# A bidirectional delta-rule scan: the two directions on separate rows of the array, four heads in one chain

## The chip, the core and the metric

The kernel runs on one core of a Trainium2 chip. Its engines are named as the profile names them: PE is TensorE (matrix products; PEld are its weight loads), DVE is VectorE, ACT is ScalarE, POOL is GpSimd, SP is SyncE. The metric is the time of one execution on the device in microseconds (us), the median of several executions; lower is better.

## What is computed

The reference is a trunk of two layers over 512 tokens of 2048 channels in float32. Each layer normalises its input, projects it by one large product, and runs two mixers beside each other: a gated delta rule in both directions over the tokens, 8 heads of 128 channels (the mixer that the change touches), and a diagonal state-space branch. Both are gated, projected, merged and projected back onto the residual.

The delta rule goes over the tokens in 8 chunks of 64. With the state S (128 x 128 for each head and direction), the triangular systems of a chunk solved beforehand, and the decays folded into the operands, one chunk is:

```python
v_new = u_c - w_c @ S                     # new values
o_c   = (q_c * exp(g)) @ S + qk_c @ v_new # outputs of the chunk
S     = S * exp(g_last) + (k_c * exp(g_last - g)).T @ v_new
...
out   = forward(q, k, v) + flip(backward(flip(q), flip(k), flip(v)))
```

## The kernel before

Activations lie channel by channel: a tile is [128 channels, 512 tokens]. The large products keep weights stationary and stream the tokens. Each float32 operand there is split into two parts, hi and lo, and a product is three instructions per contraction tile (`_steps`, lines 122 to 124, output `acc`). The parts of the weights are made by `_split`: a cast to w_hi on ACT (line 65) and a subtract to w_lo on DVE (line 66), each over 1024 columns.

The scan, `_delta_scan`, is the serial part. It runs in 16 steps per layer: two groups of four heads (hg), 8 chunks each (j); I count the steps of a layer from 0 to 15. In a step the forward direction takes chunk j and the backward direction chunk 7 - j. A chunk fills 64 of 128 rows: `half[d]` is the half of the rows in which direction d's chunk lies, and the two directions always lie in opposite halves, which change places from step to step. Before the change the four heads of a group are two chains x of two heads, and each step has these pieces:

- **ps_T** (line 807): keys and queries times the old state, for each direction and head over all 128 rows. Then r_s on DVE (line 810), v minus that, for one half at a time, and the decay of the state on DVE (line 813).
- **ps_V** (line 821): the solved triangle t_b times r_s, both directions at once. ACT copies each half into tiles v_z of its own (line 824), which are zero in the other direction's half.
- **ps_S** (line 831): the state update, tokens as contraction. All 128 rows are used, the other direction's rows of v_z being zero. DVE adds it to the state (line 836); in chunk 0 ACT copies it (line 834).
- **ps_T again** (line 839): the chunk's inner outputs are added onto the same PSUM tile, 64 columns of the array for each direction. ACT copies the result to o_tok in the first half of the chunks (line 844), DVE adds it there in the second (line 846).

Chunk 0 has no ps_T product at first, chunk 7 no state update. A float32 product of this size is two instructions on PE.

To cover the waits between the pieces, `fill.run(FILL)` puts three contraction tiles of dense products (nine instructions) between them, at three places in each step. The fills take their work from a generator: first the two last tiles of the input projection, then the eight products of the state branch's gate, then its projection. When one of the gate's products ends, ACT takes the sigmoid (line 1097), DVE multiplies twice (glu_s, line 1098; z_in, line 1099), and the result is split again (a cast on ACT, and a subtract named act on DVE, lines 65 and 66). A product of the gate has 8 contraction tiles and a step takes 9, so the ends wander through the steps.

After chunk 7 of a group, `norm` normalises the outputs of its heads on DVE and ACT; the transposes of one head at a time (ps_o) are put behind the next steps.

The order on PE within the scan is that of the code; on DVE, ACT, POOL and SP a scheduler sets it ahead of time by its own estimate, and each engine takes its instructions strictly in that order. The loads of a step (keys, values, triangles) go through POOL's DMA queue one step ahead. The PSUM pool has one buffer for each of the tiles T0, T1 (ps_T) and W0, W1 (ps_V and ps_S in turn), so a new ps_T waits until the outputs of the step before have been read.

Of the kernel before, what the change touches and what calls it, by code (L numbers as in the profile page):

```python
# [24 lines left out]
D = 2048  # L25
# [22 lines left out]
# The order of the first three products.  x: loads an input tile; h: its two parts; s: its squares;  # L48
# w j,k,n: weights of product j from contraction tile k on; p j,n: the next n steps of product j.
# [10 lines left out]
def _bc(ap, shape):  # L60
    return ap.to_broadcast(shape)
# [7 lines left out]
def _rsqrt(nc, pool, out, a, tag, bufs=None):  # L69
    """out = a ** -0.5: table root, exact reciprocal, one Newton step."""  # L70
# [32 lines left out]
class _Fill:  # L103
    """Dense products in small steps, for the places where another chain waits."""
# [11 lines left out]
def _steps(c, acc, nk, unit, hi, lo):  # L116
    """acc = w.T @ act, one contraction tile at a time; unit gives the weights from a tile on."""
# [17 lines left out]
def _sum_sq(c, ps, acc, t0, n, first):  # L135
    """Adds the sums of acc over partitions, token tiles t0 to t0 + n, onto the columns of ps [token, tile]."""
# [13 lines left out]
def _spread(c, pb, r, n):  # L150
    """pb [any partition, token] = r [token, tile]."""
# [4 lines left out]
def _rstd(c, acc, out):  # L156
    """out = (sum of acc over partitions / D + eps) ** -0.5 on every partition."""
# [8 lines left out]
def _scaled_parts(c, x, g, hi, lo):  # L166
    """Splits x*g into hi, lo."""
# [4 lines left out]
def _add_squares(c, pool, k, x, acc):  # L172
    """Adds x*x onto acc."""
# [29 lines left out]
# ---------------------------------------------------------------- decay rows  # L203
# [1071 lines left out]
```

## Time and profile before

| | us |
|---|---|
| median of 3 executions | 3102.58 (3101.16 to 3102.80) |
| the profiled execution, first to last instruction (span) | 3099.7 |
| PE busy | 3049.4 |
| DVE busy | 2307.3 |
| ACT busy | 1049.6 |
| POOL busy | 425.6 |

For the profiled execution the trace gives its span alone; the executions that are timed without the profiler have a median 2.9 us above it. Instructions on PE are pipelined, so that the durations of neighbours overlap; what a burst costs is read from start to start, or from the chain of waits, which gives each piece its own stretch. The scan of layer 0 lies at 1020 to 1216 us, that of layer 1 at 2560 to 2760 us.

### The profile page before, as it was taken

To read this page: it belongs to the slowest core of one execution; us is meant where nothing else is said; L and a number is where in the kernel's file an instruction comes from. 1 tells how busy PE (TensorE), PEld (TensorE's weight loads), DVE (VectorE), ACT (ScalarE), POOL (GpSimd) and SP (SyncE) were. 2 spreads that over 40 slices of the span, in tenths; PEclk is the share of its full clock that TensorE was granted. 3 is DMA by queue.
4 is the path that set the end of the run, shared out by engine and by line. 5 is a ranking of instruction groups with operands and counts; after the bars stand their busy time and mean duration, and the time that the engine had idled before them with its cause. 6 is when DMAs were issued, how large, how long until landed. Compare 5 with 4: busy or idle time off the path is not lost.

```text
span 3099.7 us, 45254 instructions
## 1 busy us (share of the span) xinstructions
PE 3049.4 (98%) x17142; PEld 2442.4 (79%) x17142; DVE 2307.3 (74%) x4455; ACT 1049.6 (34%) x1441; POOL 425.6 (14%) x706
## 2 busy tenths in 40 slices
PE   9999999999999999999999999999999999999998
PEld 7777788777887888888887677877778878888887
DVE  8899969997797586543487998889959965765433
ACT  4343344333222442322223334343332224423222
POOL 1010112212101231000010102022130012300000
PEclk9999999999999999999999999999999999999999
DMA  6343446755434765754433435466564356657433
GB/s 204 93 140 105 129 153 179 214 168 157 153 119 149 223 195 178 245 169 143 148 112 96 129 103 150 137 195 193 166 181 139 119 188 191 201 187 232 154 117 114
DMA packets 199289, 493.47 MB, mean 159 GB/s; under 512 B 58336, under 2 KB 62912, under 8 KB 198048
## 3 DMA queue, kind: packets, MB, share of 16 engines
q1 hardware_dynamic: 154416, 345.84, 35.1%
q0 software_dynamic: 44512, 144.74, 15.3%
q8 instruction: 135, 2.21, 0.3%
q14 instruction: 82, 0.67, 0.1%
q10 hardware_dynamic: 144, 0.01, 0.0%
HBM read 381.64 MB, written 108.86 MB: 158 GB/s over the span
## 4 chain that ended last, share of the span: by engine, by line
PE 83%; DVE 11%; issue 3%; DMA 1%; ACT 0%; POOL 0%; SPq 0%; POOLq 0%; DVEq 0%; ACTq 0%
PE acc L122 24%; PE acc L123 24%; PE acc L124 24%; DVE w_lo L66 2%; PE ps_y L271 2%; PE ps_S L831 2%; PE ps_T L807 1%; DVE st_b L482 1%; DVE st_b L481 1%; DVE h_st L484 1%; PE ps_e L271 1%; DVE cv_y L550 1%; PE ps_et L457 1%; PE ps_T L839 1%; DVE st_a L483 1%
## 5 line engine op out<-in xcount | busy, mean ns | idle before, releaser
L122 PE MATMUL acc<-act,w_hi 128*128 128x512 f32 x3200 | 1279.0, 400 | 5.5 <-DVE cv_pre L546 3.7
L124 PE MATMUL acc<-act,w_lo 128*128 128x512 f32 x3200 | 1271.6, 397 | 3.5 <-DVE w_lo L66 3.5
L123 PE MATMUL acc<-act,w_hi 128*128 128x512 f32 x3200 | 1269.6, 397 | 0.0
L65 ACT CAST w_hi<-w_raw 128x1024 fp32r<-128x1024 f32 (+1 forms) x467 | 488.2, 1046 | 1202.1 <-PE acc L123 879.9
L66 DVE TENSOR_TENSOR w_lo<-w_raw,w_hi 128x1024 fp32r<-128x1024 f32 (+1 forms) x465 | 566.7, 1219 | 266.5 <-ACT w_hi L65 264.3
L122 PEld LDWEIGHTS acc<-act,w_hi 128*128 128x128 f32 x3200 | 603.0, 188 | 150.4 <-issue 8.4
L124 PEld LDWEIGHTS acc<-act,w_lo 128*128 128x128 f32 x3200 | 602.7, 188 | 149.4 <-issue 7.0
L123 PEld LDWEIGHTS acc<-act,w_hi 128*128 128x128 f32 x3200 | 603.3, 189 | 138.4 <-issue 5.1
L122 PE MATMUL acc<-m_l,w_hi 128*128 128x512 f32 (+1 forms) x528 | 205.0, 388 | 0.0
L123 PE MATMUL acc<-m_h,w_hi 128*128 128x512 f32 (+1 forms) x528 | 204.8, 388 | 0.0
L124 PE MATMUL acc<-m_h,w_lo 128*128 128x512 f32 (+1 forms) x528 | 204.7, 388 | 0.0
L550 DVE SCALAR_TENSOR_TENSOR cv_y<-cv_pre,cw,cv_y 128x510 f32<-128x510 f32 (+1 forms) x192 | 142.6, 746 | 7.5 <-ACT cv_y L548 5.5
L122 PEld LDWEIGHTS acc<-m_l,w_hi 128*128 128x128 f32 x528 | 99.5, 188 | 21.9
L123 PEld LDWEIGHTS acc<-m_h,w_hi 128*128 128x128 f32 x528 | 99.5, 188 | 21.8
L124 PEld LDWEIGHTS acc<-m_h,w_lo 128*128 128x128 f32 x528 | 99.5, 188 | 21.8
L693 DVE TENSOR_TENSOR x_tmp<-x_inv 128x62 f32<-128x62 f32 (+30 forms) x124 | 106.3, 857 | 2.9
L695 DVE TENSOR_TENSOR x_inv<-x_inv,x_tmp 128x62 f32<-128x62 f32 (+30 forms) x124 | 106.3, 857 | 2.7
L1072 DVE TENSOR_TENSOR z_t<-acc,rstd_b 128x512 f32<-128x512 f32 x96 | 66.0, 687 | 48.2 <-PE acc L124 47.6
L1158 DVE TENSOR_TENSOR x_res<-x_res,acc 128x512 f32<-128x512 f32 x31 | 21.3, 687 | 103.7 <-PE acc L124 86.5
L1142 DVE TENSOR_TENSOR g_in<-acc,g_in 128x512 f32<-128x512 f32 x32 | 22.1, 692 | 79.4 <-PE acc L124 79.4
L518 POOL DMA_DIRECT2D m_l<-d_k x128 | 67.3, 534 | 82.2 <-PE ps_y L271 56.1
L484 DVE TENSOR_TENSOR h_st<-h_st,st_a 128x64 f32<-128x64 f32 x256 | 70.3, 275 | 5.1
(356 smaller groups left out, 3251.0 us busy)
## 6 DMA issues: line engine op xcount, KB each, us to landing
w_raw<-in_w_in_dram SPq DMA_DIRECT2D x319, 512.0 KB, 4.0
w_raw<-in_w_out_dram SPq DMA_DIRECT2D x64, 512.0 KB, 3.9
d_keqe<-k_e POOLq DMA_DIRECT2D x32, 512.0 KB, 4.5
d_g<-z_t SPq DMA_DIRECT2D x64, 256.0 KB, 2.1
w_raw<-in_w_pb_dram SPq DMA_DIRECT2D x32, 512.0 KB, 3.7
g_in<-d_g SPq DMA_DIRECT2D x64, 256.0 KB, 3.1
w_raw<-in_w_pa_dram SPq DMA_DIRECT2D x32, 512.0 KB, 4.3
ke_s<-d_keqe POOLq DMA_DIRECT2D x56, 256.0 KB, 4.1
```

What stands on the lines that cost most here:

```text
L65: nc.scalar.copy(out=hi, in_=src)
L66: nc.vector.tensor_tensor(out=lo, in0=src, in1=hi.bitcast(F32), op=ALU.subtract)
L122: c.nc.tensor.matmul(acc, wh[:, q, :], lo(k), start=k == 0, stop=False)
L123: c.nc.tensor.matmul(acc, wh[:, q, :], hi(k), start=False, stop=False)
L124: c.nc.tensor.matmul(acc, wl[:, q, :], hi(k), start=False, stop=k == nk - 1)
L271: c.nc.tensor.matmul(out[r], w[:, r], x, start=start, stop=stop)
L484: V.tensor_tensor(out=hs(n + 1), in0=hs(n + 1), in1=a, op=ALU.add)
L518: c.q.dma_start(out=M[s_ * 16:(s_ + 1) * 16].rearrange("p g t c -> p g (t c)"), in_=c.d_k[l][j][:, :, 0:16, (7 - s_) * 16:(15 - s_) * 16]. ...
L550: nc.vector.scalar_tensor_tensor(out=y[:, o0:o1], in0=pre[:, i0:i0 + o1 - o0], scalar=cw[:, tap:tap + 1], in1=y[:, o0:o1], op0=ALU.mult, o ...
L693: V.tensor_tensor(out=t, in0=_bc(X[:, k + 1:, k:k + 1], [128, n, k]), in1=_bc(X[:, k:k + 1, 0:k], [128, n, k]), op=ALU.mult)
L695: V.tensor_tensor(out=X[:, k + 1:, 0:k], in0=X[:, k + 1:, 0:k], in1=t, op=ALU.add)
L1072: V.tensor_tensor(out=z, in0=acc, in1=c.rstd, op=ALU.mult)
```

## The change

Three things change in `_delta_scan`, and `norm` is written for the new tiles.

1. The two chains of two heads become one of four. The tiles of the state, of r_s, of the new values, of ps_T, ps_V and ps_S now hold four heads, and each step issues half as many instructions on DVE and ACT, of twice the columns.
2. The state product and the inner outputs take only the 64 rows in which the direction's chunk lies (`half[d]`), so that the two directions stand on different rows of the array. The zeroed tiles v_z and their memsets go; ps_V is copied in one piece to v_n.
3. ps_T and ps_S have a PSUM bank for each direction. The banks in use stay four: two for T, two for W.

The number of products is the same. Comments and docstrings are gone from the whole file, which moves line numbers: line 836 of before is 821 after, 846 is 831, 810 is 803, 831 is 817, 839 is 824.

```diff
     V = nc.vector
     HL = [slice(0, 64), slice(64, 128)]
-    NC = 2
+    H4 = 4
     with ExitStack() as es:
         psp = es.enter_context(tc.tile_pool(name=f"sps_{l}", bufs=1, space=PSUM, reuse_waits="tile"))
         tp = es.enter_context(tc.tile_pool(name=f"st_{l}", bufs=1, side="right", reuse_waits="tile"))
         wk = es.enter_context(tc.tile_pool(name=f"sw_{l}", bufs=2, side="right", reuse_waits="tile"))
-        tb = [tp.tile([128, 4, 128], F32, name=f"t_b{q}") for q in range(2)]
-        # new values, zero in the half of the other direction
-        vz = [[[tp.tile([128, 2, 128], F32, name=f"v_z{x}{d}{p}") for p in range(2)] for d in range(2)] for x in range(NC)]
-        Sg = [[tp.tile([128, 2, 2, 128], F32, name=f"s_st{hg}{x}") for x in range(NC)] for hg in range(2)]
-        og = [[tp.tile([128, 4, 2, 128], F32, name=f"o_tok{hg}{x}") for x in range(NC)] for hg in range(2)]
-        for q in tb + [vz[x][d][p] for x in range(NC) for d in range(2) for p in range(2)]:
+        tb = [tp.tile([128, H4, 128], F32, name=f"t_b{q}") for q in range(2)]
+        Sg = [tp.tile([128, 2, H4, 128], F32, name=f"s_st{hg}") for hg in range(2)]
+        og = [tp.tile([128, 4, H4, 128], F32, name=f"o_tok{hg}") for hg in range(2)]
         def norm(hg):
...
+            ot = og[hg]
+            ms = tp.tile([128, 4, H4], F32, name=f"o_ms{hg}")
...
         late = []
         ahead = load(*steps[0])
         for s, (hg, j) in enumerate(steps):
             S, ot = Sg[hg], og[hg]
-            p = j % 2
             n_, t_, half = where(j)
             T, ke, ld = ahead
             if s + 1 < len(steps):
                 ahead = load(*steps[s + 1])
-            pT, rr, vv = [], [], []
-            for x in range(NC):
-                g0 = hg * 4 + 2 * x
-                ps = psp.tile([128, 2, 2, 128], F32, name=f"ps_T{x}", tag=f"T{x}")
-                r = wk.tile([128, 2, 128], F32, name=f"r_s{x}", tag=f"r_s{x}", bufs=1)
+            hs = slice(hg * 4, hg * 4 + 4)
+
+            ps = psp.tile([128, 2, H4, 128], F32, name="ps_T", tag="T")
+            r = wk.tile([128, H4, 128], F32, name="r_s", tag="r_s", bufs=1)
+            for d in range(2):
                 if j == 0:
-                    # the state is zero
+
+                    V.tensor_copy(out=r[half[d]], in_=ld[d][2][half[d]])
+                else:
+                    for h in range(H4):
+                        nc.tensor.matmul(ps[:, d, h, :], ke[d][:, h, :], S[:, d, h, :],
+                                         start=h == 0, stop=True, skip_group_check=True)
+                    V.tensor_tensor(out=r[half[d]], in0=ld[d][2][half[d]], in1=ps[half[1 - d], d], op=ALU.subtract)
+            if 0 < j < NCH - 1:
+                V.tensor_tensor(out=S, in0=S, in1=_bc(c.egl[:, :, hs, j:j + 1], [128, 2, H4, 128]), op=ALU.mult)
+            fill.run(FILL)
+            pv = psp.tile([128, H4, 128], F32, name="ps_V", tag="W")
+            for h in range(H4):
+                nc.tensor.matmul(pv[:, h, :], T[:, h, :], r[:, h, :], start=True, stop=True)
+            vv = wk.tile([128, H4, 128], F32, name="v_n", tag="v_n")
+            nc.scalar.copy(out=vv, in_=pv)
+            fill.run(FILL)
+            if j < NCH - 1:
+                pS = psp.tile([128, 2, H4, 128], F32, name="ps_S", tag="W")
+                for h in range(H4):
                     for d in range(2):
-                        V.tensor_copy(out=r[half[d]], in_=ld[d][2][half[d], 2 * x:2 * x + 2])
+                        nc.tensor.matmul(pS[:, d, h, :], ld[d][1][half[d], h, :], vv[half[d], h, :], start=True, stop=True)
+                if j == 0:
+                    nc.scalar.copy(out=S, in_=pS)
                 else:
-                    for d in range(2):
-                        for h in range(2):
-                            nc.tensor.matmul(ps[:, d, h, :], ke[d][:, 2 * x + h, :], S[x][:, d, h, :],
-                                             start=d == 0 and h == 0, stop=True, skip_group_check=True)
-                    for d in range(2):
-                        V.tensor_tensor(out=r[half[d]], in0=ld[d][2][half[d], 2 * x:2 * x + 2],
-                                        in1=ps[half[1 - d], d], op=ALU.subtract)
-                    if j < NCH - 1:
-                        V.tensor_tensor(out=S[x], in0=S[x], op=ALU.mult,
-                                        in1=_bc(c.egl[:, :, g0:g0 + 2, j:j + 1], [128, 2, 2, 128]))
-                pT.append(ps)
-                rr.append(r)
-            fill.run(FILL)
-            for x in range(NC):
-                pv = psp.tile([128, 2, 128], F32, name=f"ps_V{x}", tag=f"W{x}")
-                for h in range(2):
-                    nc.tensor.matmul(pv[:, h, :], T[:, 2 * x + h, :], rr[x][:, h, :], start=True, stop=True)
-                vv.append([vz[x][d][p] for d in range(2)])
+                    V.tensor_tensor(out=S, in0=S, in1=pS, op=ALU.add)
+            for h in range(H4):
                 for d in range(2):
-                    nc.scalar.copy(out=vv[x][d][half[d]], in_=pv[half[d]])
-            fill.run(FILL)
-            for x in range(NC):
-                if j < NCH - 1:
-                    ps = psp.tile([128, 2, 2, 128], F32, name=f"ps_S{x}", tag=f"W{x}")
-                    for d in range(2):
-                        for h in range(2):
-                            nc.tensor.matmul(ps[:, d, h, :], ld[d][1][:, 2 * x + h, :], vv[x][d][:, h, :],
-                                             start=True, stop=True)
-                    if j == 0:
-                        nc.scalar.copy(out=S[x], in_=ps)
-                    else:
-                        V.tensor_tensor(out=S[x], in0=S[x], in1=ps, op=ALU.add)
-                for h in range(2):
-                    for d in range(2):
-                        nc.tensor.matmul(pT[x][half[d], d, h, :], ld[d][0][:, 2 * x + h, :],
-                                         vv[x][d][:, h, :], start=j == 0 and h == 0, stop=True, skip_group_check=True)
-                for d in range(2):
-                    o = ot[x][half[d], t_[d]]
-                    if j < NCH // 2:
-                        nc.scalar.copy(out=o, in_=pT[x][half[d], d])
-                    else:
-                        V.tensor_tensor(out=o, in0=o, in1=pT[x][half[d], d], op=ALU.add)
+                    nc.tensor.matmul(ps[half[d], d, h, :], ld[d][0][half[d], h, :], vv[half[d], h, :],
+                                     start=j == 0 and h == 0, stop=True, skip_group_check=True)
+            for d in range(2):
+                o = ot[half[d], t_[d]]
+                if j < NCH // 2:
+                    nc.scalar.copy(out=o, in_=ps[half[d], d])
+                else:
+                    V.tensor_tensor(out=o, in0=o, in1=ps[half[d], d], op=ALU.add)
             fill.run(FILL)
             if late:
                 late.pop(0)()
```

On PE, in step 0 of layer 0, between the second fill and the third (v_z and v_n are the new values, kd_s the keys of one direction, a_s its inner attention). Before:

```order
L831 MATMUL ps_S_9521<-v_z_9330,kd_s_9357 128x128 x2
L831 MATMUL ps_S_9521<-v_z_9332,kd_s_9363 128x128 x2
L839 MATMUL ps_T_9475<-v_z_9330,a_s_9359 64x128
L839 MATMUL ps_T_9475<-v_z_9332,a_s_9365 64x128
L839 MATMUL ps_T_9475<-v_z_9330,a_s_9359 64x128
L839 MATMUL ps_T_9475<-v_z_9332,a_s_9365 64x128
L831 MATMUL ps_S_9533<-v_z_9334,kd_s_9357 128x128 x2
L831 MATMUL ps_S_9533<-v_z_9336,kd_s_9363 128x128 x2
L839 MATMUL ps_T_9484<-v_z_9334,a_s_9359 64x128
```

After, the end of the state burst and the start of the outputs:

```order
L817 MATMUL ps_S<-v_n,kd_s_9337 128x128
L817 MATMUL ps_S<-v_n,kd_s_9343 128x128
L817 MATMUL ps_S<-v_n,kd_s_9337 128x128
L817 MATMUL ps_S<-v_n,kd_s_9343 128x128
L824 MATMUL ps_T<-v_n,a_s_9339 64x128
L824 MATMUL ps_T<-v_n,a_s_9345 64x128
L824 MATMUL ps_T<-v_n,a_s_9339 64x128
```

State and output bursts stood twice in turn, each over two heads; now one of eight state products is followed by one of eight outputs, and the directions alternate in both.

On DVE, in step 4 of layer 0, behind the decay of the state (o_tok are the outputs, s_st the state). Before:

```order
L66 TENSOR_TENSOR w_lo<-w_raw,w_hi 128x1024
L1098 TENSOR_TENSOR glu_s<-glu_s,ys_in 128x512
L836 TENSOR_TENSOR s_st_9337<-s_st_9337,ps_S_9869 128x512
L846 TENSOR_TENSOR o_tok_9341<-o_tok_9341,ps_T_9806 64x256 x2
L1099 TENSOR_TENSOR z_in<-z_in,glu_s 128x8x64
L836 TENSOR_TENSOR s_st_9338<-s_st_9338,ps_S_9881 128x512
L846 TENSOR_TENSOR o_tok_9342<-o_tok_9342,ps_T_9815 64x256 x2
```

After:

```order
L66 TENSOR_TENSOR w_lo<-w_raw,w_hi 128x1024
L1083 TENSOR_TENSOR glu_s<-glu_s,ys_in 128x512
L1084 TENSOR_TENSOR z_in<-z_in,glu_s 128x8x64
L821 TENSOR_TENSOR s_st_9329<-s_st_9329,ps_S 128x1024
L831 TENSOR_TENSOR o_tok_9331<-o_tok_9331,ps_T 64x512 x2
L66 TENSOR_TENSOR act_9661<-z_in,act_9659 128x512
```

The first chain's state sum and outputs stood ahead of z_in; now the whole sum and both output adds stand behind it.

On DVE, in step 9 of layer 0, from the end of a gate product on. Before:

```order
L1098 TENSOR_TENSOR glu_s<-glu_s,ys_in 128x512
L810 TENSOR_TENSOR r_s_10390<-v_s_10118,ps_T_10389 64x256
L810 TENSOR_TENSOR r_s_10390<-v_s_10124,ps_T_10389 64x256
L813 TENSOR_TENSOR s_st_9339<-s_st_9339,egl 128x512
L810 TENSOR_TENSOR r_s_10399<-v_s_10118,ps_T_10398 64x256
L810 TENSOR_TENSOR r_s_10399<-v_s_10124,ps_T_10398 64x256
L813 TENSOR_TENSOR s_st_9340<-s_st_9340,egl 128x512
L1099 TENSOR_TENSOR z_in<-z_in,glu_s 128x8x64
```

After:

```order
L1083 TENSOR_TENSOR glu_s<-glu_s,ys_in 128x512
L803 TENSOR_TENSOR r_s<-v_s_10015,ps_T 64x512
L1084 TENSOR_TENSOR z_in<-z_in,glu_s 128x8x64
L66 TENSOR_TENSOR act_9661<-z_in,act_9659 128x512
L803 TENSOR_TENSOR r_s<-v_s_10021,ps_T 64x512
L805 TENSOR_TENSOR s_st_9330<-s_st_9330,egl 128x1024
```

All four subtracts stood ahead of z_in; now z_in and the rounding (act) stand between the subtracts of the two directions. In layer 1 the rounding stands behind the second one.

## Rows read from the trace of the kernel before

**Rows 1.** Page, section 1 (engine busy us, share of span, instructions) and the clock row of section 2.
```profile
PE 3049.4 (98%) x17142; PEld 2442.4 (79%) x17142; DVE 2307.3 (74%) x4455; ACT 1049.6 (34%) x1441; POOL 425.6 (14%) x706
...
PEclk9999999999999999999999999999999999999999
```

**Rows 2.** Chain of waits, 1060 to 1120 us: start us, us, engine, tile, line, instructions.
```profile
1072.21 1.78 PE ps_T L807 x16
...
1076.08 0.89 PE ps_V L821 x8
...
1079.07 0.89 PE ps_S L831 x8
1079.96 0.59 PE ps_T L839 x8
1080.55 1.09 PE ps_S L831 x8
1081.63 0.59 PE ps_T L839 x8
...
1084.51 2.00 PE ps_T L807 x16
...
1088.62 0.89 PE ps_V L821 x8
...
1100.93 0.89 PE ps_V L821 x8
...
1116.23 1.02 PE ps_T L839 x16
```

**Rows 3.** Groups by line, DVE and ACT: shapes, count | busy us, mean ns | idle before.
```profile
L810 DVE TENSOR_TENSOR r_s<-v_s,ps_T 64x256 f32<-64x256 f32 x112 | 47.0, 420 | 27.6 <-PE ps_T L807 24.8 <-DMA a_s<-d_a 0.2
...
L836 DVE TENSOR_TENSOR s_st<-s_st,ps_S 128x512 f32<-128x512 f32 x48 | 32.9, 685 | 34.2 <-PE ps_S L831 33.7
...
L773 DVE TENSOR_TENSOR o_tok<-o_tok,o_f 128x1024 f32<-128x1024 f32 x8 | 9.8, 1221 | 0.1
...
L824 ACT COPY v_z<-ps_V 64x256 f32<-64x256 f32 x128 | 46.9, 366 | 64.5 <-PE ps_V L821 62.2
...
L834 ACT COPY s_st<-ps_S 128x512 f32<-128x512 f32 x8 | 4.7, 585 | 4.9 <-PE ps_S L831 4.8
```

**Rows 4.** Timelines, steps 3 to 5 of layer 0: start us, us, engine, instruction [idle before].
```profile
1062.11 0.62 ACT L65 CAST act<-ys_in 128x512 fp32r<-128x512 f32 x1 [3.71 <-DMA ys_in<-d_y]
...
1075.92 1.05 PE L821 MATMUL ps_V<-r_s,t_b 128*128 128x128 f32 x8
...
1078.18 1.05 ACT L65 CAST w_hi<-w_raw 128x1024 fp32r<-128x1024 f32 x1
...
1079.26 1.22 DVE L66 TENSOR_TENSOR w_lo<-w_raw,w_hi 128x1024 fp32r<-128x1024 f32 x1 [2.92 <-ACT w_hi L65]
...
1082.48 1.27 DVE L1099 TENSOR_TENSOR z_in<-z_in,glu_s 128x512 f32<-128x512 f32 x1
...
1093.19 0.69 DVE L66 TENSOR_TENSOR act<-z_in,act 128x512 fp32r<-128x512 f32 x1
```

**Rows 5.** Timelines, step 9 of layer 0.
```profile
1132.97 0.85 DVE L810 TENSOR_TENSOR r_s<-v_s,ps_T 64x256 f32<-64x256 f32 x2
...
1134.22 0.60 PE L821 MATMUL ps_V<-r_s,t_b 128*128 128x128 f32 x4
...
1135.38 0.71 PE L821 MATMUL ps_V<-r_s,t_b 128*128 128x128 f32 x4 [0.56 <-DVE r_s L810]
```

**Rows 6.** Timeline of PE, step 10 of layer 0.
```profile
1147.79 0.61 PE L821 MATMUL ps_V<-r_s,t_b 128*128 128x128 f32 x4
...
1149.25 0.71 PE L821 MATMUL ps_V<-r_s,t_b 128*128 128x128 f32 x4 [0.85 <-DVE r_s L810]
```

**Rows 7.** Windows: stretch us, us, each engine's busy us (instructions), PEclk, DMA share, GB/s.
```profile
1700.00:2000.00 300.00, 287.11 (x1739) 225.34 (x1738) 267.80 (x666) 109.43 (x143) 41.18 (x72) 0.98 0.41 130
2000.00:2300.00 300.00, 295.19 (x1938) 230.10 (x1939) 266.95 (x627) 109.38 (x145) 76.25 (x111) 1.00 0.61 182
```

More of the change, by code (lines that the diff above doesn't have):

```diff
@@ L714, in _delta_scan @@
         wk = es.enter_context(tc.tile_pool(name=f"sw_{l}", bufs=2, side="right", reuse_waits="tile"))
-        tb = [tp.tile([128, 4, 128], F32, name=f"t_b{q}") for q in range(2)]
-        vz = [[[tp.tile([128, 2, 128], F32, name=f"v_z{x}{d}{p}") for p in range(2)] for d in range(2)] for x in range(NC)]
-        Sg = [[tp.tile([128, 2, 2, 128], F32, name=f"s_st{hg}{x}") for x in range(NC)] for hg in range(2)]
-        og = [[tp.tile([128, 4, 2, 128], F32, name=f"o_tok{hg}{x}") for x in range(NC)] for hg in range(2)]
-        for q in tb + [vz[x][d][p] for x in range(NC) for d in range(2) for p in range(2)]:
+        tb = [tp.tile([128, H4, 128], F32, name=f"t_b{q}") for q in range(2)]
+        Sg = [tp.tile([128, 2, H4, 128], F32, name=f"s_st{hg}") for hg in range(2)]
+        og = [tp.tile([128, 4, H4, 128], F32, name=f"o_tok{hg}") for hg in range(2)]
+        for q in tb:
             nc.gpsimd.memset(q, 0.0)
@@ L755, in norm @@
         def norm(hg):
-            late = []
-            for x in range(NC):
-                g0 = hg * 4 + 2 * x
-                ot = og[hg][x]
-                ms = tp.tile([128, 4, 2], F32, name=f"o_ms{hg}{x}")
-                for t in range(2):
-                    sq = wk.tile([128, 2, 2, 128], F32, name="o_sq", tag=f"o_sq{t}", bufs=1)
-                    nc.scalar.activation(out=sq, in_=ot[:, 2 * t:2 * t + 2], func=AF.Square)
-                    V.tensor_reduce(out=ms[:, 2 * t:2 * t + 2], in_=sq, axis=AX.X, op=ALU.add)
-                rq = c.rq[:, :, g0:g0 + 2]
-                f = tp.tile([128, 4, 2], F32, name=f"o_f{hg}{x}")
-                V.tensor_tensor(out=f, in0=rq, in1=rq, op=ALU.mult)
-                V.tensor_tensor(out=f, in0=f, in1=ms, op=ALU.mult)
-                V.tensor_scalar(out=f, in0=f, scalar1=1.0 / 128, scalar2=EPS, op0=ALU.mult, op1=ALU.add)
-                _rsqrt(nc, tp, ms, f, f"o_rt{hg}{x}")
-                V.tensor_tensor(out=f, in0=ms, in1=rq, op=ALU.mult)
-                V.tensor_tensor(out=ot, in0=ot, in1=_bc(f.unsqueeze(3), [128, 4, 2, 128]), op=ALU.mult)
-                def head(ot=ot, g0=g0, h=0):
-                    pt = c.psq.tile([128, 4, 128], F32, name="ps_o", tag="psq")
-                    for t in range(4):
-                        nc.tensor.transpose(pt[:, t, :], ot[:, t, h, :], c.ident)
-                    of = wk.tile([128, 4, 128], F32, name="o_t", tag=f"o_sq{h}", bufs=1)
-                    nc.vector.tensor_scalar(out=of, in0=pt, scalar1=c.hng, scalar2=None, op0=ALU.mult)
-                    c.q.dma_start(out=c.d_o[l][g0 + h], in_=of.rearrange("p t x -> p (t x)"))
-                late += [lambda h=h, f=head: f(h=h) for h in range(2)]
@@ L784, in norm @@
-            return late
+            ot = og[hg]
+            ms = tp.tile([128, 4, H4], F32, name=f"o_ms{hg}")
+            for t in range(4):
+                sq = wk.tile([128, H4, 128], F32, name="o_sq", tag=f"o_sq{t % 2}", bufs=1)
+                nc.scalar.activation(out=sq, in_=ot[:, t], func=AF.Square)
+                V.tensor_reduce(out=ms[:, t], in_=sq, axis=AX.X, op=ALU.add)
+            rq = c.rq[:, :, hg * 4:hg * 4 + 4]
+            f = tp.tile([128, 4, H4], F32, name=f"o_f{hg}")
@@ new lines, in norm @@
+            V.tensor_tensor(out=f, in0=rq, in1=rq, op=ALU.mult)
+            V.tensor_tensor(out=f, in0=f, in1=ms, op=ALU.mult)
+            V.tensor_scalar(out=f, in0=f, scalar1=1.0 / 128, scalar2=EPS, op0=ALU.mult, op1=ALU.add)
+            _rsqrt(nc, tp, ms, f, f"o_rt{hg}")
+            V.tensor_tensor(out=f, in0=ms, in1=rq, op=ALU.mult)
+            for h in range(0, H4, 2):
+                V.tensor_tensor(out=ot[:, :, h:h + 2], in0=ot[:, :, h:h + 2],
+                                in1=_bc(f[:, :, h:h + 2].unsqueeze(3), [128, 4, 2, 128]), op=ALU.mult)
@@ new lines, in head @@
+            def head(h):
+                pt = c.psq.tile([128, 4, 128], F32, name="ps_o", tag="psq")
+                for t in range(4):
+                    nc.tensor.transpose(pt[:, t, :], ot[:, t, h, :], c.ident)
+                of = wk.tile([128, 4, 128], F32, name="o_t", tag=f"o_sq{h % 2}", bufs=1)
+                nc.vector.tensor_scalar(out=of, in0=pt, scalar1=c.hng, scalar2=None, op0=ALU.mult)
+                c.q.dma_start(out=c.d_o[l][hg * 4 + h], in_=of.rearrange("p t x -> p (t x)"))
@@ L786, in _delta_scan @@
+            return [lambda h=h: head(h) for h in range(H4)]
         late = []
@@ L794, in _delta_scan @@
                 ahead = load(*steps[s + 1])
-            pT, rr, vv = [], [], []
-            for x in range(NC):
-                g0 = hg * 4 + 2 * x
-                ps = psp.tile([128, 2, 2, 128], F32, name=f"ps_T{x}", tag=f"T{x}")
-                r = wk.tile([128, 2, 128], F32, name=f"r_s{x}", tag=f"r_s{x}", bufs=1)
-                if j == 0:
+            hs = slice(hg * 4, hg * 4 + 4)
+            ps = psp.tile([128, 2, H4, 128], F32, name="ps_T", tag="T")
+            r = wk.tile([128, H4, 128], F32, name="r_s", tag="r_s", bufs=1)
```

1 line of the change is left out of this document (removed).

## Prediction

> **What bounds the kernel now.** I read the page first. TensorE is busy for 98% of the span, VectorE for 74%, ScalarE for 34%, and the granted clock stands at its full level (2.4 GHz) in every slice [rows 1]. So the array is the bound, and the scan is no exception: in the chain of waits through its first steps every piece belongs to PE [rows 2]. The second view is that chain, read for its lengths. From one ps_V burst to the next it is 12.31 us (1088.62 to 1100.93), and the pieces add up to it: ps_T 1.78, a fill of nine products 2.09 (1073.99 to 1076.08), ps_V 0.89, a fill 2.10 (1076.97 to 1079.07), then state and output bursts in turn, 0.89 + 0.59 + 1.09 + 0.59 = 3.16, and the way to the next ps_T 2.29, which is a fill and 0.19 for the return to the full array. Anything taken off those bursts comes off the time, as long as VectorE and ScalarE still deliver between them. The third view, the timelines of VectorE and ScalarE [rows 4 to 6], is for that condition.
>
> **Part 1, the state bursts on separate rows.** Before, a state product ran over all 128 rows with the other direction's half zeroed, 16 instructions to a step, 0.111 us apart (8 in 0.89 us [rows 2]). Now the two directions use different 64 rows and stand in turn, d0, d1, d0, d1; each writes its own PSUM bank. No row of this trace shows two products on different rows. The nearest is the output burst, whose two directions stand in turn on different columns: 16 instructions in 1.02 us, the change of shape included, where 16 in the full array take 1.78 [rows 2]. That is pairs side by side. Bounds: side by side, the 16 take 8 x 0.111 = 0.89; one after the other, 1.78. I take 0.89, because the column case is the same array, type and length, and alternates in the same way.
>
> The rule for it: the Trainium skill, TensorEngine Tiling (Array Packing), Key Properties, says that different tiles load weights and multiply in parallel. The Trainium skill, TensorE: Matmul & The Clock Gate, Measured speedup vs the span model, gives 3.07 times for four row tiles; that share (77%) on two tiles would make the 0.89 about 1.16, an estimate, and the time some 7.6 us longer than my sum. No run here shows it yet.
>
> **Part 2, fewer changes of shape.** Before, each step alternates state, output, state, output; now it is one state and one output burst (the first order listing). A second state burst behind an output burst costs 1.09 instead of 0.89 [rows 2], so a change to a new shape costs about 0.2. The state burst now has a shape of its own, entered from the fill: 0.89 + 0.20 = 1.09. The outputs, 64 rows by 64 columns, still lie in disjoint columns: 1.02 as in the step that has outputs alone. The return, 0.19, was there before. So 1.09 + 1.02 = 2.11 for 3.16: **1.05 us off a step**. States are updated in 7 of 8 chunks, two head groups, two layers: 28 steps, **29.4 us**. The four last chunks have outputs alone, 1.02 before and after. If the entries cost 0.1 more or less, that is 3 us either way. ps_T and ps_V keep their number and shape.
>
> **Part 3, the coarser chain on VectorE and ScalarE.** A 64x256 subtract takes 0.42, 128x512 0.69, 128x1024 1.22 [rows 3], so a pass over twice the columns costs about 0.27 (256 columns) or 0.53 (512) more, not double: per step two subtracts at an estimated 0.69 for four at 0.42, one state product and one state sum at 1.22 each for two each at 0.69. VectorE has less work. ScalarE copies the new values in one 128x512 copy, 0.59 as the state copy of that size, for four at 0.37. All this lies beside PE and saves nothing by itself. But there was slack in the two chains: the second one's results were needed 0.89 us later than the first one's. Now the first ps_T waits for the sum of all four heads, and ps_V for both subtracts, while PE reaches ps_T 1.05 us sooner. What waits, step by step (a layer's steps are 0 to 15):
>
> - Before: 0.23 in step 4 (12.54 to the next ps_V for 12.31 [rows 2]); 0.7 and 1.0 in steps 9 and 10, where the second half of ps_V starts at 1135.38 and 1149.25 instead of 0.44 us behind the first [rows 5, 6]. About 1.95 a layer, 3.9 in all.
> - Step 4 after: the order puts w_lo, the gate and z_in ahead of the one state sum (second listing). w_hi starts at 1078.18 when the four copies are through [rows 4]; behind one short copy it can start some 0.4 sooner. Then w_lo stands at 1078.85, the gate 1.15 later at 1080.0, z_in at 1080.65, the sum 1.3 later at 1081.95, and the two o_tok adds end at 1084.5 (1.22, then twice 0.69, a little overlapped). PE is at ps_T at 1075.92 [rows 4] + 0.89 + 2.10 + 2.11 + 0.19 + 2.10 = 1083.3: a wait of 1.2. Step 5, where the rounding of the activations (act) stands ahead of the sum as well, from 1093.19 [rows 4]: sum at 1093.85, adds through at 1096.4, ps_T due 7.39 behind this step's ps_V (1088.62, less the 0.16 by which the chain's pieces stand behind the starts), at 1095.85: 0.55. Step 6: none. Behind the late ps_T stand only PE's own next products; nobody else hurries.
> - Step 9 after: in layer 0, z_in and the act rounding stand between the two subtracts (third listing). First subtract 1132.97 to 1133.6, z_in to 1134.8, ScalarE's cast to 1135.45, act to 1136.1, second subtract to 1136.75; ps_V is due at 1134.22 [rows 5]: 2.6. In layer 1 only z_in stands there: 1.25. Step 10: 0.4 in both.
> - Step 3: an act rounding whose cast waits for a DMA now stands between the subtracts; 0.7 as a guess between 0 and 3, since ScalarE waits 3.71 us for that load before [rows 4].
>
> That makes 5.45 and 4.1, together 9.55, against 3.9: **5.6 us lost**. From below it could be zero waits (3.9 gained), from above three times mine (15 lost).
>
> **Part 4, what is moved elsewhere.** The eight memsets of zero halves go from POOL; PE does not wait for them (before the first ps_V it runs fills). The loads of a step stay the same transfers on POOL's queue. In layer 1 the scheduler also deals the state branch and the value products in another order from about 1880 us on. PE idles 12.9 and 4.8 us in the two windows that hold this [rows 7]; the first gap there (around 1743 us, with the drop of the clock to a mean of 0.98) has the same order on VectorE as before, so it stays. I take nothing for the rest, between -4 and +4.
>
> **Sum.** Span 3099.7 - 29.4 + 5.6 = 3075.9; runs without the profiler have a median 2.9 above this span (3102.58), so 3078.8, say 3079.
>
> **Rivals.**
> - *State pairs do not run side by side* (the change does not do what it says on rows), outputs still do through their columns. Then the state burst is 1.78 + 0.20 and a step saves 0.16, 4.5 in all; ps_T is due 0.89 later, so the waits of steps 4 and 5 nearly go and about 6.9 stay, 3 more than before: about 3101. For it: no row shows row pairs. Against: the column pairs.
> - *Products on different rows exclude each other altogether*, the outputs too, which lose the pairing that they have now, because their directions now sit on different rows. State 1.98, outputs 1.02 + 0.87 = 1.89: 3.87 for 3.16, +0.71 in 28 steps and +0.87 in four, 23.4, and 2 for waits: about 3128, slower. It decides as soon as the two bursts together exceed 3.16.
> - *The chain becomes the bound*: the waits are three times mine (every step from 3 to 10 catches VectorE in front of a sum or a second subtract). For it: VectorE at 74%, 5 to 6 us of fill work in a step's queue. Against: in steps 0 to 2 and 11 to 15 no gate work stands in front. Then 3078.8 + 19 = 3098.
> - *No new waits*: the order's late subtracts fall into the fills. 3078.8 - 9.5 = 3069.
>
> **How the numbers follow.** 0.2% (6.2 us) is about what a measurement of this kernel can tell from no change. My forecast, 3072 to 3088, has 0.66; no new waits 0.09; chain as the bound 0.08; no pairs of states 0.11; rows excluding each other 0.06. Range 3068 to 3098: it takes in the forecast, no waits and most of the third rival. Faster 0.82 (the first three, less a little of the third), same 0.12, slower 0.06.
>
> **What would show it.** In the profile after: the starts of the state burst in pairs and the burst at about 1.1 us for 16 instructions; outputs at about 1.0; steps 1, 2 and 12 to 14 of each layer at 11.26 us; PE's waits on VectorE in front of ps_T in steps 4 and 5, in front of ps_V in 9 and 10. I am wrong in the mechanism if the state burst takes over 1.6 us, in the size if PE waits in the scan exceed 15 us, and in neither if the difference comes from 1700 to 2300 us.

## The result and the profile after: 20 us slower

The changed kernel takes 3122.85 us (median; 3122.21 to 3123.96), the kernel before 3102.69 beside it: ratio 1.0066, 95% interval 1.0055 to 1.0078. The forecast was 3079 us, with a range of 3068 to 3098. The change costs 20 us where I expected it to save 24, and the time lies outside the range.

The profiled execution has a span of 3121.4 us for 3099.7, 21.7 more. Page, sections 1 and 2, of the kernel after (engine, busy us, share of the span, instructions), to be held against [rows 1]:

```profile
PE 3033.9 (97%) x17142; PEld 2419.1 (77%) x17142; DVE 2287.6 (73%) x4275; ACT 1018.0 (33%) x1308; POOL 423.4 (14%) x690
...
PEclk9999999999999999999999999999999999999999
```

PE is busy 15.5 us less than before, in a span that is 22 us longer: what was saved in work came back as idle time, and more of it. Of the 22, 17.3 lie between the first and the last ps_V of the two scans (386.5 us for 369.2), and 3.8 between the scans. Where in the scans, the list of PE's waits inside the scan of layer 0 says (engine, tile, line, what it waited for: us in total, times, longest; "issue" is idle time for which the profile shows no cause). Before, in the same scan:

```profile
PE ps_V L821 <- DVE r_s L810: 1.4, 2, 0.8
```

After:

```profile
PE ps_T L801 <- DVE r_s L803: 16.1, 14, 2.7
PE ps_T L801 <- issue: 1.3, 2, 0.7
PE ps_T L801 <- ACT o_tok L829: 0.8, 1, 0.8
PE ps_o L776 <- DVE o_tok L770: 0.4, 1, 0.4
```

Fourteen waits, one in each step that has ps_T products, of products for a *subtract*; over both layers 28 with 32.1 us. Before, ps_T never waited for r_s there; only ps_V did. The timelines of PE and DVE show the pattern where no filler work of DVE stands in the way; I call such a step clean. A step is measured here from its ps_V to the next one, so that the ps_T at its end is that of the following step: these lines run from the state burst of step 12 of layer 0 to ps_V of step 13 (start us, us, engine, line, operation, tiles, shapes, count, idle before):

```profile
1187.89 1.16 PE L817 MATMUL ps_S<-v_n,kd_s 64*128 64x128 f32 x16
1188.98 1.09 PE L824 MATMUL ps_T<-v_n,a_s 64*64 64x128 f32 x16
1190.01 0.50 PE L122 MATMUL acc<-act,w_hi 128*128 128x512 f32 x1
...
1192.20 1.05 PE L801 MATMUL ps_T<-s_st,ke_s 128*128 128x128 f32 x8
1194.03 1.16 PE L801 MATMUL ps_T<-s_st,ke_s 128*128 128x128 f32 x8 [0.77 <-DVE r_s L803]
1194.94 0.47 PE L122 MATMUL acc<-act,w_hi 128*128 128x512 f32 x1
...
1197.12 1.05 PE L809 MATMUL ps_V<-r_s,t_b 128*128 128x128 f32 x8
```
```profile
1193.29 0.68 DVE L803 TENSOR_TENSOR r_s<-v_s,ps_T 64x512 f32<-64x512 f32 x1 [1.68 <-PE ps_T L801]
1195.23 0.69 DVE L803 TENSOR_TENSOR r_s<-v_s,ps_T 64x512 f32<-64x512 f32 x1 [1.25 <-PE ps_T L801]
```

And the same burst before:

```profile
1182.81 1.95 PE L807 MATMUL ps_T<-s_st,ke_s 128*128 128x128 f32 x16
1184.51 0.47 PE L122 MATMUL acc<-act,w_hi 128*128 128x512 f32 x1
```

The bursts that the change was about came out as forecast: 16 state products in 1.09 us (1187.89 to 1188.98), 16 outputs in 1.03, together 2.12 for the 3.16 of [rows 2]. But ps_T, which ran as 16 in 1.70, now runs as 8, a pause, and 8: 2.74 (1192.20 to 1194.94). The pause ends 0.06 after direction 0's subtract (1193.29 + 0.68 = 1193.97). So 1.04 is lost where 1.04 was gained, and this step is 12.31 long in both kernels. In steps with filler work on DVE the subtract comes later and the pause is longer. The list of the semaphores that an instruction waits for, in the program, says the same: in step 1 the first product of direction 1 has a semaphore of DVE now, which it had not before. (DMASW4_49 is a load's semaphore, DVE_49 VectorE's.)

```
before: L807 MATMUL ps_T<-s_st,ke_s 128x128 [waits DMASW4_49]
after:  L801 MATMUL ps_T<-s_st,ke_s 128x128 [waits DMASW4_49,DVE_49]
```

The code says why. Before, the loop over directions with the products stood ahead of the loop with the subtracts. After, one loop holds both: products of 0, subtract of 0, products of 1, subtract of 1, all on one tile `ps_T` of two banks. Direction 1's products write a bank that direction 0's subtract never reads, but the tile is the same.

### The profile page after: what moved, and what is told of

It reads as the page before. It is cut to its first block, busy times and chain, and to the rows that moved or that the text cites. A ratio compares the mean times of both kernels' runs of the same rounds, so it can differ in the third digit from the quotient of the medians.

```text
span 3121.4 us, 44831 instructions
## 1 busy us (share of the span) xinstructions
PE 3033.9 (97%) x17142; PEld 2419.1 (77%) x17142; DVE 2287.6 (73%) x4275; ACT 1018.0 (33%) x1308; POOL 423.4 (14%) x690
## 3 DMA queue, kind: packets, MB, share of 16 engines
q0 software_dynamic: 44512, 144.74, 15.1%
## 5 line engine op out<-in xcount | busy, mean ns | idle before, releaser
L801 PE MATMUL ps_T<-s_st,ke_s 128*128 128x128 f32 x448 | 63.6, 286 | 35.6 <-DVE r_s L803 32.1
L801 PEld LDWEIGHTS ps_T<-s_st,ke_s 128*128 128x128 f32 x448 | 56.0, 194 | 44.9 <-DVE r_s L803 37.5
```

The lines of the kernel that those rows point to most:

```text
L801: nc.tensor.matmul(ps[:, d, h, :], ke[d][:, h, :], S[:, d, h, :], start=h == 0, stop=True, skip_group_check=True)
```

## Experiments

**Theory A**: the waits come from the order of writing on a shared tile, and take all that was to be gained. **Theory B**: the chain of four heads is too coarse for VectorE and ScalarE, and would wait elsewhere if not there. **Theory C**: the loss is in the middle of layer 1, where the order of other work was dealt anew. The ratios below are to the kernel before, which took 3101.8 to 3101.9 us in these series; differences to the changed kernel go from one series to another, in which the kernel before differs by 0.9.

### The products first

```diff
+            for d in range(2 if j else 0):
+                for h in range(H4):
+                    nc.tensor.matmul(ps[:, d, h, :], ke[d][:, h, :], S[:, d, h, :],
+                                     start=h == 0, stop=True, skip_group_check=True)
             for d in range(2):
                 if j == 0:
                     V.tensor_copy(out=r[half[d]], in_=ld[d][2][half[d]])
                 else:
-                    for h in range(H4):
-                        nc.tensor.matmul(ps[:, d, h, :], ke[d][:, h, :], S[:, d, h, :],
-                                         start=h == 0, stop=True, skip_group_check=True)
                     V.tensor_tensor(out=r[half[d]], in0=ld[d][2][half[d]], in1=ps[half[1 - d], d], op=ALU.subtract)
```

> The changed kernel, with all eight ps_T products of both directions written ahead of both subtracts; nothing else moves. Theory A (the second direction's products wait for the first direction's subtract): the 0.96 us go from each of 28 steps, 27 us, and with them most of the 10 us by which 32.1 us of these waits exceed 28 x 0.78; waits of up to 10 us in front of ps_T or ps_V may take their place. Then 3084 to 3096 us. Theory B (the single chain of four heads is too coarse for VectorE and ScalarE, wherever it waits): the idle time moves from the second products to ps_V, and the time stays at 3112 to 3123. Theory C (other work in the middle of layer 1, where the order was dealt anew): no more than 4 us of the loss belong to the scan's products, above 3115.

Measured: 3078.2 us, ratio 0.9925 (0.991 to 0.994). The two ps_T halves are one burst again and nothing waits for r_s there. The bursts of a step like the one above (fills left out; the window ends within the last burst), and PE's waits in this scan:

```profile
1163.47 1.05 PE L810 MATMUL ps_V<-r_s,t_b 128*128 128x128 f32 x8
1166.55 1.16 PE L818 MATMUL ps_S<-v_n,kd_s 64*128 64x128 f32 x16
1167.64 1.09 PE L825 MATMUL ps_T<-v_n,a_s 64*64 64x128 f32 x16
1170.86 1.95 PE L797 MATMUL ps_T<-s_st,ke_s 128*128 128x128 f32 x16
1174.74 0.49 PE L810 MATMUL ps_V<-r_s,t_b 128*128 128x128 f32 x3
```
```profile
PE ps_T L797 <- issue: 1.3, 2, 0.7
PE ps_o L776 <- DVE o_tok L770: 0.5, 1, 0.5
PE ps_V L810 <- DVE r_s L804: 0.4, 1, 0.4
```

A step is 11.27 (1163.47 to 1174.74). Moving the products ahead gives back 44.7 us, more than the 27 plus most of 10 that I wrote down: the time is 6 us below the range that I gave. B and C fall as main causes. In the two scans 43.3 us come back: 29.1 are 28 x 1.04 (I had counted 0.96); 10.3 are the rest of the 32.1 beyond 28 x 0.78; and 4.9 are the clock. That last term shows in the windows of the kernel after (stretch, us, busy us of each engine with instructions, PEclk, DMA share, GB/s), three of its long steps and the clean one:

```profile
1065.10:1080.20 15.10, 13.50 (x85) 10.99 (x85) 9.28 (x11) 5.18 (x8) 5.03 (x9) 0.89 1.06 276
1127.40:1144.30 16.90, 13.78 (x88) 11.08 (x87) 14.28 (x23) 8.98 (x13) 3.99 (x7) 0.90 0.56 168
2695.00:2710.20 15.20, 13.33 (x89) 10.94 (x88) 8.42 (x10) 3.90 (x6) 5.04 (x9) 0.90 0.63 201
1197.10:1209.40 12.30, 11.52 (x84) 9.58 (x83) 7.72 (x10) 2.92 (x4) 1.25 (x2) 1.00 0.50 156
```

15.1 x 0.11 + 16.9 x 0.10 + 15.2 x 0.10 = 4.9, an estimate from means that are rounded. These terms make 44.3 for 43.3. The 1.0 left over I did not assign; this version has waits of its own that the kernel after has not.

### A tile for each direction

```diff
-            ps = psp.tile([128, 2, H4, 128], F32, name="ps_T", tag="T")
+            ps = [psp.tile([128, H4, 128], F32, name=f"ps_T{d}", tag=f"T{d}") for d in range(2)]
```

(and `ps[d][...]` for `ps[..., d, ...]` in the four places that use it; the order of writing is that of the changed kernel.)

> The changed kernel in its own written order (products of direction 0, its subtract, products of direction 1, its subtract), but ps_T is two tiles of one bank each, one for each direction, in the same four banks. Theory A says that the wait comes from the shared tile, not from the banks or from the engines: it goes here as in the version with the products first, and the time agrees with that within 4 us (3082 to 3096); the first subtract may start up to 0.9 us earlier in a step, which counts only where ps_V waits. If the wait came from the two directions' products and a read of PSUM getting in each other's way, it would stay: 3118 to 3125.

Measured: 3076.21 us, ratio 0.9918 (0.9903 to 0.9932), the fastest version of the study: 26 us faster than the kernel before and 47 than the changed one. It agrees with the products first within 4 us, as expected; both lie below the range that I gave. PE's waits in the scan of layer 0:

```profile
PE ps_o L776 <- DVE o_tok L770: 0.5, 1, 0.5
PE ps_V L809 <- DVE r_s L803: 0.4, 1, 0.4
```

With the same banks, written order and engines, the wait is gone. In its program, in the step of the list of waits above, the first product of direction 1 waits for a load and for ACT, which read the outputs of the step before, and no longer for DVE. So it was neither the bank nor the engines but the tile, as the unit in which the program holds a write against earlier reads. This version is 2 us ahead of the one with the products first, whose list has two waits of 0.66 ("issue") ahead of ps_T that are not here: steps 4 and 5 take 11.44 here and 12.15 there. A ps_T of one tile has to wait until both directions' outputs of the step before have been read, one of two tiles only for its own; that this is the reason was not tried by itself.

The Trainium skill, PSUM — Partial Sum Buffer, PSUM bank collisions raise a hardware error, asks for a guard by bank and quadrant. By that rule direction 1's products need not wait for a read of the other bank; the runs agree: the wait that cost 29 us and more was no need of the memory.

### The same order of writing in the kernel before

```diff
                     for d in range(2):
                         for h in range(2):
                             nc.tensor.matmul(ps[:, d, h, :], ke[d][:, 2 * x + h, :], S[x][:, d, h, :],
                                              start=d == 0 and h == 0, stop=True, skip_group_check=True)
-                    for d in range(2):
                         V.tensor_tensor(out=r[half[d]], in0=ld[d][2][half[d], 2 * x:2 * x + 2],
                                         in1=ps[half[1 - d], d], op=ALU.subtract)
```

> The kernel before with one edit: in each of its two chains the subtract of direction 0 is written between the products of direction 0 and those of direction 1, which lie in one tile. Theory A: each chain's second products wait for a subtract of 0.42 plus 0.32 on the way there and 0.06 on the way back, less the 0.11 pitch: 0.69; in the second chain VectorE's decay of the first chain's state (0.69) stands in front, less the 0.02 it overlaps: 1.36. 2.05 in 24 steps, 1.38 in four, 54.7 us, and up to 8 more where filler work of VectorE falls between the subtracts: 3155 to 3166. If the written order of products and subtracts does not matter, 3100 to 3106.

Measured: 3197.01 us, ratio 1.0309 (1.0291 to 1.0326): 95 slower than before, on a kernel without a single row pair or longer chain. The sign and the place are A's; the loss is half as much again as the highest that I gave (64 over the kernel before). Both directions of a chain share one bank in this kernel, so the run shows what the written order costs, and does not tell the tile from the bank; the version with two tiles does that. Its waits in layer 0's scan, and two windows that hold the scans of this kernel:

```profile
PE ps_T L807 <- DVE r_s L809: 29.4, 28, 2.5
```
```profile
1020.00:1262.00 242.00, 212.61 (x1276) 176.28 (x1275) 128.87 (x221) 78.33 (x154) 52.27 (x92) 0.94 0.51 153
2611.00:2848.00 237.00, 207.57 (x1265) 171.99 (x1264) 128.37 (x221) 76.98 (x150) 52.28 (x92) 0.95 0.51 154
```

The scan of layer 0 in the kernel before:

```profile
1020.00:1216.00 196.00, 194.59 (x1295) 165.04 (x1294) 130.42 (x225) 78.75 (x156) 51.99 (x92) 1.00 0.64 192
```

Over both layers these waits are 56 with 58.8 us, about what I had. The greater part of what is missing is the clock: 0.94 and 0.95 in the mean, where the scan of the kernel before runs at 1.00, cost 242 x 0.06 + 237 x 0.05 = 26 us, an estimate. The remaining 10 fit what the products lose when a burst starts anew after each pause, 0.2 a time. That was not measured by itself; a step at clock 1.00 (from 1214.93 us) is 14.46 long for 12.31, with 1.6 of waits, which leaves 0.27 for each of its two pauses.

### The state products on all rows

The version with the products first, but with the zeroed tiles of the kernel before:

```diff
-            nc.scalar.copy(out=vv, in_=pv)
+            vv = [vz[d][j % 2] for d in range(2)]
+            for d in range(2):
+                nc.scalar.copy(out=vv[d][half[d]], in_=pv[half[d]])
...
-                        nc.tensor.matmul(pS[:, d, h, :], ld[d][1][half[d], h, :], vv[half[d], h, :], start=True, stop=True)
+                        nc.tensor.matmul(pS[:, d, h, :], ld[d][1][:, h, :], vv[d][:, h, :], start=True, stop=True)
```

> The version with the products first, but the state products run over all 128 rows with the other direction's rows of the new values zeroed, as in the kernel before (two copies of 64 rows by ScalarE for one of 128); the outputs keep their 64 rows. If the row pairs are worth what the trace after shows (16 instructions in 1.09 us with the entry, against 1.78), this is 28 x 0.69 = 19.3 us slower than the version with the products first, or 16 to 20 where shorter waits give some back. If the pairs gain nothing that reaches the end, the two agree within 4 us.

Measured: 3095.94 us, ratio 0.998 (0.9971 to 0.999): 17.7 slower than the version with the products first. Its state burst, on PE:

```profile
1173.96 1.95 PE L820 MATMUL ps_S<-v_z,kd_s 128*128 128x128 f32 x16
1175.84 1.09 PE L827 MATMUL ps_T<-v_z,a_s 64*64 64x128 f32 x16
1176.86 0.50 PE L122 MATMUL acc<-act,w_hi 128*128 128x512 f32 x1
```

1.88 to the outputs for 1.09, with the fill behind them at 2.90 for 2.12. A clean step is 11.97 for 11.27. So the row pairs are worth about 18 us; one chain and fewer changes of shape, without the pairs, the other 6.

### A fill between the directions

```diff
                     V.tensor_tensor(out=r[half[d]], in0=ld[d][2][half[d]], in1=ps[half[1 - d], d], op=ALU.subtract)
+                    if d == 0:
+                        fill.run(1)
...
-            fill.run(FILL)
+            fill.run(FILL - 1 if j else FILL)
```

> The changed kernel with its shared tile and its written order, so with the wait; but of the three contraction tiles that fill the time behind ps_T one (three products, 0.70 us) now stands between the products of direction 0 and the subtract's successor, the products of direction 1. Theory A as I now hold it (the loss is idle time of PE, because nothing stands behind the first direction's products): a clean step has 1.06 to cover (0.32, 0.68, 0.06) and 0.70 to cover it with, so 0.3 stays, 11.6 us a step, 8 us in 28 steps, and 3 to 10 where filler work of VectorE stands between the subtracts: 3086 to 3098. If the loss were in the two subtracts lying apart, whatever PE does meanwhile, it would stay above 3112.

Measured: 3102.43 us, ratio 0.9999 (0.999 to 1.0008). The three products that stand in the pause give back 20 of the 45 us, with the order of products and subtracts as it was, which speaks for idle PE as the loss; but the time is 4 us above my range. Clean steps are 11.60, as forecast. The waits that the profile lists are where filler work of DVE stands ahead of the first subtract, not between the two: 1.2 to 2.0 in each of steps 8 to 10 of both layers, 0.2 to 0.65 in steps 0, 1 and 5, together 11.3 for the 3 to 10 that I gave to filler work. ps_V, which now has a third less fill ahead of it, waits three times in a layer, 1.8 in all; that I had not counted.

### The bursts cut in two again

The version with two tiles, with states and outputs in turn for two heads each, as before:

```diff
-                for h in range(H4):
-                    for d in range(2):
-                        nc.tensor.matmul(pS[:, d, h, :], ld[d][1][half[d], h, :], vv[half[d], h, :], start=True, stop=True)
...
             for h in range(H4):
+                if j < NCH - 1 and h % 2 == 0:
+                    for g in (h, h + 1):
+                        for d in range(2):
+                            nc.tensor.matmul(pS[:, d, g, :], ld[d][1][half[d], g, :], vv[half[d], g, :], start=True, stop=True)
                 for d in range(2):
                     nc.tensor.matmul(ps[d][half[d], h, :], ld[d][0][half[d], h, :], vv[half[d], h, :],
```

> The version with a tile for each direction, with the state and output bursts cut in two again, as in the kernel before: states of heads 0 and 1, their outputs, states of heads 2 and 3, their outputs; same instructions. By part 2 of the prediction a change of shape costs 0.15 to 0.2, and two more of them are made in each of 28 steps: (0.44 + 0.20 + 0.59) x 2 = 2.46 for 2.11, 0.35 a step, 9.8 us, and about 1 for the state sum, whose last product comes 0.6 later: 3085 to 3089. If changes of shape cost nothing, 3075 to 3078.

Measured: 3080.73 us, ratio 0.9931 (0.9918 to 0.9945), 4.5 above the uncut version. The four bursts on PE:

```profile
1169.79 0.71 PE L819 MATMUL ps_S<-v_n,kd_s 64*128 64x128 f32 x8
1170.44 0.65 PE L821 MATMUL ps_T<-v_n,a_s 64*64 64x128 f32 x8
1171.02 0.71 PE L819 MATMUL ps_S<-v_n,kd_s 64*128 64x128 f32 x8
1171.66 0.66 PE L821 MATMUL ps_T<-v_n,a_s 64*64 64x128 f32 x8
```

0.65, 0.58, 0.64 and 0.59 (to the fill at 1172.25) make the 2.46 that was forecast, and a clean step is 11.61, 0.34 more. That is 9.5 us in 28 steps; the end shows 4.5. (The profiled executions differ by 5.6: 9.2 more in the scans, 2.8 less between them, 0.6 less ahead of them.) So most of the rest lies outside the scan, and answers theory C: from the last ps_V of layer 0 to the first of layer 1 this version takes 1356.6, the uncut one 1359.4 and the changed kernel 1360.2, the kernel before 1356.4. Of these only the cut one has, between the scans, PE's products in the order of the kernel before; the uncut and the changed kernel have the new one. The other versions, the kernel before with the new order of writing among them, all have the new one too, and take 1359.0 to 1360.4. The windows of uncut, cut, after and before:

```profile
1197.10:2556.50 1359.40, 1336.86 (x7303) 1062.51 (x7302) 1017.35 (x1974) 440.89 (x552) 155.87 (x246) 1.00 0.48 154
```
```profile
1201.50:2558.10 1356.60, 1337.15 (x7303) 1061.27 (x7303) 1017.12 (x1974) 438.29 (x549) 155.36 (x246) 1.00 0.48 154
```
```profile
1221.80:2582.00 1360.20, 1337.82 (x7303) 1061.11 (x7302) 1017.62 (x1974) 440.85 (x552) 155.93 (x246) 1.00 0.48 154
```
```profile
1211.30:2567.70 1356.40, 1337.08 (x7304) 1060.86 (x7303) 1019.00 (x1989) 440.05 (x554) 157.37 (x254) 1.00 0.49 154
```

PE has the same work in all four (1337 busy) and idles some 3 us more in the new order. So C is real, at 3 to 4 us, and no more, one profiled execution of each kernel taken. Which of the pieces that changed places costs them was not tried.

### Outputs in the shape of the states

The version with two tiles, outputs with weights padded by zeros to 128 columns:

```diff
-                    A = wk.tile([128, 4, CH], F32, name=f"a_s{d}", tag=f"a_s{d}")
-                    c.q.dma_start(out=A, in_=c.d_a[l][d, t, :, hs, :])
+                    A = ab[d][j // 2 % 2]
+                    for q in range(2):
+                        c.q.dma_start(out=A[HL[q], :, q * 64:q * 64 + 64], in_=c.d_a[l][d, t, HL[q], hs, :])
...
-                    nc.tensor.matmul(ps[d][half[d], h, :], ld[d][0][half[d], h, :], vv[half[d], h, :],
+                    nc.tensor.matmul(ps[d][:, h, :], ld[d][0][half[d], h, :], vv[half[d], h, :],
```

> The version with a tile for each direction, with the outputs' weights padded by zeros to 128 columns (the padded operand is loaded in two pieces for each direction), so that the outputs run in the same shape as the states, 64 rows by 128 columns, and the change between the two bursts goes. If that change costs 0.15 even between two shapes of 64 rows, a step saves 0.15, 4 us in 28 steps: 3071 to 3074. If outputs cost more because they now write all 128 partitions, or the loads in smaller pieces make a step wait, 3077 to 3085.

Measured: 3078.84 us, ratio 0.9924 (0.9911 to 0.9938). A clean step does get shorter, 11.13 for 11.27, but nothing of it reaches the end. A wait ahead of ps_V of step 3, of 1.74 us in layer 0 and 1.66 in layer 1, is new; so is one of 0.6 in each layer ahead of ps_T, at the end of step 4, for DVE's sums of the outputs. PE, then DVE, then ACT there:

```profile
1062.31 0.94 PE L811 MATMUL ps_V<-r_s,t_b 128*128 128x128 f32 x6 [1.74 <-DVE r_s L805]
```
```profile
1057.62 0.68 DVE L805 TENSOR_TENSOR r_s<-v_s,ps_T 64x512 f32<-64x512 f32 x1 [0.16 <-PE ps_T L803]
1060.84 0.69 DVE L66 TENSOR_TENSOR act<-ys_in,act 128x512 fp32r<-128x512 f32 x1 [2.53 <-ACT act L65]
1061.57 0.69 DVE L805 TENSOR_TENSOR r_s<-v_s,ps_T 64x512 f32<-64x512 f32 x1
```
```profile
1060.19 0.62 ACT L65 CAST act<-ys_in 128x512 fp32r<-128x512 f32 x1 [4.27 <-DMA ys_in<-d_y]
```

The order now has a rounding of the activations between the two subtracts; it waits for a cast, which waits for a load. This is the step 3 risk that the prediction put at 0.7, at 1.74, in a kernel whose order on DVE fell out differently.

## Why the prediction was wrong

**Part 1, right.** Two products on different rows run side by side: 0.89 + 0.20 forecast, 1.09 measured; worth 17.7 us by itself. The Trainium skill, TensorE: Matmul & The Clock Gate, Measured speedup vs the span model, gives 3.07 times for four row tiles. My estimate from it for two tiles, 1.16 for 0.89, was too high for this shape: with the entry it would make 1.36, and the trace has 1.09. No run here has four row tiles.

**Part 2, right in its sum, wrong in its last sentence.** 2.11 forecast, 2.12 measured, 1.05 off a step, and cutting the bursts again cost 0.34 a step where my figures gave 0.35. But "ps_T and ps_V keep their number and shape" was taken to mean that they keep their time. This is the step that failed. Number and shape were kept, and what stood between the products changed: a read of the same tile, by another engine. ps_T took 2.74 for 1.70. That cost 1.04 a step, 29.1 us, and 10 and 5 more with late subtracts and the clock, and I had it at nothing, though the order of writing could be read in the diff.

**Part 3, sized on the wrong base.** I counted waits of ps_T for the state sum and of ps_V for the subtracts, with ps_T due as one burst. In the version with the products first, where that holds, the steps beyond 11.27 (with the transposes' 0.44 in steps 8 to 11 taken out) give 3.6 and 3.8 us a layer, 7.4 for my 9.55. Steps 4 and 5 have 0.88 each, for 1.2 and 0.55; step 6 has 0.28 and step 3 0.2 to 0.3 ahead of the next ps_T, for none. The 0.7 ahead of ps_V of step 3 is not there, and of the 0.4 of step 10 0.1 is left. Step 8 has 1.3: in it ps_o waits 0.50 for DVE, which I had missed, and ps_V of step 9 waits 0.43 for its subtract, where I had put 2.6 and 1.25: without the wait the order puts z_in behind both subtracts. The third order listing ahead of the prediction, with z_in and act between two subtracts, was thus a sign of the fault: with the wait work is dealt into that place, and in both versions without the wait it is not. I read it as a cost, and did not ask why it had room there.

**Part 4, inside its bounds.** Taken as 0 within -4 to +4; 3.8 in the changed kernel, between the scans.

**The rivals.** None named it. 3122.85 comes near the 3128 of "rows exclude each other", whose mechanism is refuted. "The chain becomes the bound" had the right sign of waits, but on ps_V and state sums, and at 19 us. The sum was good for another kernel: 3075.9 of span forecast, 3076.2 measured with the products first. That it agrees to 0.3 is partly luck, since there the scans came out 2.2 us better than the sum and the stretch between them 3.3 worse. The text's own test of size, PE waits in the scan above 15 us, fired at 32.1; it would have called the miss one of size, and it was a wait that the sum did not have.

## What to carry to other kernels

Ask of a change not only what each instruction costs, but what now stands between two of them on the same tile: in this kernel products that are written behind a read of their tile wait for it, even where they touch another bank of it. List the semaphores that each instruction on the bound engine waits for, before and after, and explain every new one. If a tile is shared by two streams, write all producers ahead of all consumers, or give each stream a tile of its own.

## What was not expected of the hardware

Short pauses were paid a second time, through the clock. PE in the kernel before with the new order of writing, after a pause of 0.52 us and one of 1.24:

```profile
1238.94 1.16 PE L807 MATMUL ps_T<-s_st,ke_s 128*128 128x128 f32 x8 [0.52 <-DVE r_s L809]
1241.34 0.99 PE L807 MATMUL ps_T<-s_st,ke_s 128*128 128x128 f32 x4 [1.24 <-DVE r_s L809]
1241.98 0.78 PE L122 MATMUL acc<-act,w_hi 128*128 128x512 f32 x1
1242.55 0.63 PE L123 MATMUL acc<-act,w_hi 128*128 128x512 f32 x1
1242.98 0.63 PE L124 MATMUL acc<-act,w_lo 128*128 128x512 f32 x1
```

The dense products start 0.43 us apart there for 0.23 elsewhere, and the granted clock of such clean steps is 0.89 to 0.90 in the mean, so a part of them is at the lower of the two levels (1.2 for 2.4 GHz). It does not follow each such pair: in that kernel about every second clean step has it. Over both scans this was some 26 us by the estimate above, against 59 of idle time.
